# A chunk pipeline split into a front and a rear line, in the projection stage of a hybrid encoder layer

## The chip, the cores and the metric

The kernel runs on one NeuronCore of one Trainium2 chip. The metric is the device time of one execution in microseconds. Before the change three runs took 1786.5 to 1789.83 us, median 1787.34 us.

## The reference, cut to what matters

One layer of an encoder, 1024 positions of width 1024. RMSNorm, one combined projection to 26 column tiles of 128, two groups of heads that read it, an output projection, a second norm and an MLP. Tiles 0 to 11 are q, k and v of the attention heads; tiles 12 to 25 feed the recurrent heads.

```python
h = _rms_norm(x, ln1_g); proj = h @ w_in
q, k, v, u = proj[..., :512], proj[..., 512:1024], proj[..., 1024:1536], proj[..., 1536:]
attn = _dilated_window_attention(q, k, v, q_g, k_g)     # q and k are RMS-normed per head of 64
rwkv = _rwkv7_bidirectional(u, ...)                     # below
x = x + concat([attn, rwkv]) @ w_out
x = x + square(relu(_rms_norm(x, ln2_g) @ w_up)) @ w_down
...
for direction, reverse in ((0, False), (1, True)):
    decay = exp(-exp(-softplus(-(w0 + tanh(xw) @ w2)) - 0.5)); a = sigmoid(a0 + xa @ a2)
    kt = k * (1 + (a - 1) * k_a)
    # S_t = S_{t-1} (diag(w_t) - kk_t^T (a_t kk_t)) + v_t^T k_t ;  y_t = S_t r_t
    ys.append(_wkv7_scan(r, decay, kt, v, kk, a, reverse))
```

The scan is done in 16 chunks of 64 positions. What does not depend on the state (products within a chunk, the inverse of a 64x64 triangular system, values scaled by running decays) is prepared for all chunks ahead, and a short recurrence over chunks follows.

## The kernel before, in words

The kernel is one program in a framework that keeps the written order as a priority: a planner places each instruction on its engine by dependencies, buffers and that order, and each engine then runs its own queue strictly in order. DMAs are issued from the queues of SP, ScalarE (ACT) and GpSimd (POOL).

**Three stages.** `in_proj` (L164 to L635) makes the projection and the chunk preparation; `mixers` (L839 to L981) runs the recurrence over chunks with attention beside it; `tail` (L984 on) is the output projection and the MLP, 128x512 matmuls one after another.

**The dense filler.** Generator `dense` (L353) goes through the 26 column tiles in `order`. `proj` (L275) does one tile: per half of 512 positions 24 matmuls of 128x512 (three products of a high and low split, eight blocks of the contraction), with a `yield` after every six. I call six such matmuls a dense step. A half ends in `evac`: for the recurrent tiles one multiply (L308), for q and k a norm in place (L318 to L333: scale, Square on ACT, `head_inv` with eight small matmuls and a reciprocal, `head_rep` with a Sqrt on ACT and four transposes, a multiply, a split, two DMAs), for v four transposes and two DMAs (L338 to L350).

**The chunk units.** For each of four head pairs `p` and each half `hf`: `per_half` (L415) makes the normalised key `kkn`, the transposed values `VT` and the decay gate `om`; then for each direction `d` `unit_a` (L447) makes th, the exponentials EE and Ei, the scaled operands `al` and `bk` (L472 to L484), the 128x128 products `psg` (L496), masked to `G` by VectorE (L501), DMAs of G to `gd` and `rec_dr`, transposes `psb` (L508), copies `BK` (L512) and a DMA on the ACT queue (L513). `bonus` (L582) closes a half. `bk` holds three blocks per chunk; the third is a copy by ACT (L482) for the upper 64 partitions.

**The triangular systems.** When both halves of a (p, d) are done, `pair_b` (L520) goes on a list `back`: it loads the 16x16 diagonal blocks `MP` from `gd`, inverts them in 15 VectorE steps (L534, L536), stores them (`td`), and then per half loads `Ab`, `t16`, `t16t` and runs `unit_c` (L556): four rounds of 32 matmuls of 64x64 into the one bank `psd` (L564), each followed by a VectorE operation that the next round needs. The two halves run one after the other.

**The pacing.** `drive` (L386) advances a chunk generator one `yield` at a time; after each it advances `back` by 0.6 of a step and the dense filler by 0.7. `until` (L381) runs the filler until a tile is there. When all chunks are out, L630 to L633 run each remaining `back` step with four dense steps; then the stage's pools are closed and `mixers` starts, where `fill(20, 4.7)` (L965) gives each of 16 chunk steps up to 20 dense steps if any are left, else 4.7 pieces of attention.

**PSUM.** Eight banks: three `pa` for the dense accumulators, shared with the norms' and v's small products (`psq`); two `pm` (`pse`) for the chunk units' small products; two `pg` (`psg`, `psb`); one `pd` (`psd`).

Of the kernel before, what the change touches and what calls it, by code (L numbers as in the profile page):

```python
# [8 lines left out]
F32 = mybir.dt.float32  # L9
# [38 lines left out]
def tile_trunk(ctx: ExitStack, tc: tile.TileContext, xT, w_in, w_o, w_up, w_dn, vecs, w2w0, a2, g2, cst, att,  # L48
# [82 lines left out]
    def head_rep(rn, sp, pp):  # L131
        rx = sp.tile([P, 8, 64], F32, name="rx", tag="rx")
        nc.scalar.activation(rx, rn.rearrange("p (i o) -> p i o", o=1).to_broadcast([P, 8, 64]), AF.Sqrt)
        psb = pp()
        for t in range(4):
            nc.tensor.transpose(psb[:, t * P:(t + 1) * P], rx[:, 2 * t:2 * t + 2].rearrange("p h x -> p (h x)"), ident)
        return psb
# [26 lines left out]
    def in_proj():  # L164
        with ExitStack() as st:
# [24 lines left out]
            def prefetch():  # L190
                i = len(raws)
                if i < len(order):
                    r = []
                    for j in range(2):
# [5 lines left out]
                     [pa[0].tile([P, 512], F32, name="ps_u", tag="acc"), pd.tile([P, 512], F32, name="ps_u", tag="psd")],  # L200
                     [pg.tile([P, 512], F32, name="ps_u", tag="psg") for _ in range(2)]]
# [114 lines left out]
            def qk_tile(p, which):  # L316

                def evac(hf, ps):  # L318
# [9 lines left out]
                    hi = tq.tile([P, 512], F32R, name="qhi", tag="qt")  # L328
                    nc.scalar.copy(hi, qc)
                    lo = tq.tile([P, 512], F32R, name="qlo")  # L330
                    nc.vector.tensor_sub(lo, qc, r2f(hi))
                    nc.sync.dma_start((qh_dr, kh_dr)[which][p][:, sl], r2f(hi))
                    nc.sync.dma_start((ql_dr, kl_dr)[which][p][:, sl], r2f(lo))  # L333
                yield from proj(4 * which + p, evac)

            def v_tile(p):

                def evac(hf, ps):  # L338
# [4 lines left out]
                    ps = pq()  # L343
                    for t in range(4):
                        nc.tensor.transpose(ps[:, t * P:(t + 1) * P], vc[:, t * P:(t + 1) * P], ident)
                    vn = tq.tile([P, 4, 2, 65], F32, name="vn", tag="qt")
                    nc.gpsimd.memset(vn[:, :, :, 64:65], 1.0)
                    nc.scalar.copy(vn[:, :, :, 0:64], ps.rearrange("p (t h e) -> p t h e", t=4, h=2))
                    for h in range(2):
                        nc.sync.dma_start(v_dr[p][h, sl].rearrange("(t p) f -> p t f", p=P), vn[:, :, h])  # L350
                yield from proj(8 + p, evac)

            def dense():  # L353
                for c in order:
# [6 lines left out]
                    T.setdefault(c - 12, None)  # L361
# [5 lines left out]
            filler = dense()  # L367
# [18 lines left out]
            def drive(g, rate):  # L386

                while True:
                    try:
                        next(g)  # L390
                    except StopIteration as e:
                        return e.value
                    behind(0.6)
                    credit[0] += rate
                    while credit[0] >= 1.0:
                        credit[0] -= 1.0
                        next(filler, None)
# [17 lines left out]
            def per_half(w):  # L415
# [5 lines left out]
                rn = head_inv(sq, 1.0, 1e-12, up, pp)  # L421
                kkn = w["kkn"] = up.tile([P, 512], F32, name="kkn")
                nc.vector.scalar_tensor_tensor(kkn, kr[:, sl], V("kk", p), head_rep(rn, up, pp), ALU.mult, ALU.mult)
# [23 lines left out]
            def unit_a(u, w, d):  # L447
# [24 lines left out]
                al = up.tile([P, 8, 2, 64], F32, name="al")  # L472
                bk = up.tile([P, 8, 3, 64], F32, name="bk")
# [7 lines left out]
                nc.vector.scalar_tensor_tensor(bk[:, :, 0], v3(tm), 0.5, Ei, ALU.mult, ALU.mult)  # L481
                nc.scalar.copy(bk[64:128, :, 2], bk[64:128, :, 0])  # L482
                nc.vector.tensor_mul(kt, kt, kr[:, sl])
                nc.vector.tensor_mul(bk[:, :, 1], v3(kt), Ei)  # L484
                yield
                w["kt"].append(kt)
                for h in range(2):
                    nc.gpsimd.dma_start(rec_dr[d][H[h], cs, p, h * P:h * P + 64], al[H[h], :, 0])
                    nc.gpsimd.dma_start(rec_dr[d][H[h], cs, p, 448 + h * 64:512 + h * 64], al[H[h], :, 1])
                gd = dr.tile([64, 1040], F32, name=f"gd{u}")  # L490
                Gs = [up.tile([P, 8, P], F32, name="G", bufs=2) for h in range(2)]
                for g in range(2):
                    pss = [pg.tile([P, 4, P], F32, name="psg") for h in range(2)]
                    for c in range(4):
                        for h in range(2):
                            nc.tensor.matmul(pss[h][:, c], bk[H[h], 4 * g + c, h:h + 2].rearrange("p a b -> p (a b)"),  # L496
                                             al[H[h], 4 * g + c].rearrange("p a b -> p (a b)"), start=True, stop=True)
                    yield
                    for h in range(2):
                        gm = K(f"gm{'fb'[d]}{h}").rearrange("p (o x) -> p o x", o=1)  # L500
                        nc.vector.tensor_mul(Gs[h][:, 4 * g:4 * g + 4], pss[h], gm.to_broadcast([P, 4, P]))  # L501
# [698 lines left out]
```

## Time and profile before

The profiled execution took 1784.77 us, of which the span of the core's instructions is 1783.0 us and 1.77 us lie around it. Stages by the granted clock and by how much of each engine is busy (us; the windows are cut at the first products of the recurrence and at the start of the uninterrupted tail):

| stretch | length | PE | DVE | ACT | POOL | granted clock | DMA share |
|---|---|---|---|---|---|---|---|
| 0 to 60, start | 60 | 48.5 | 37.0 | 29.9 | 15.8 | 0.97 | 0.56 |
| 60 to 612, projection and chunks | 552 | 479.8 | 334.0 | 201.7 | 100.0 | 0.89 | 0.70 |
| 612 to 960, recurrence and attention | 348 | 308.1 | 191.9 | 145.1 | 64.5 | 0.93 | 0.86 |
| 960 to 1010, end of attention | 50 | 45.7 | 28.4 | 20.4 | 11.2 | 0.87 | 0.57 |
| 1010 to 1783, tail | 773 | 767.5 | 270.6 | 146.4 | 102.6 | 1.00 | 0.16 |

PE is TensorE, DVE VectorE. "Busy" is time in which an instruction of the engine was running; the clock is the mean share of full speed that TensorE was granted; the DMA share is the mean busy share of the core's 16 DMA engines.

### The profile page before, as it was taken

How to read it: one execution, taken by the hardware profiler on the slowest of the kernel's cores; microseconds unless marked ns; L12 is line 12 of the kernel's file. 1: busy time of each engine (PE TensorE's matmuls, PEld its weight loads, DVE VectorE, ACT ScalarE, POOL GpSimd, SP SyncE). 2: the span in 40 equal slices, each digit the busy share in tenths (PEclk: the TensorE clock that was granted, in tenths of full speed). 3: DMA queues.
4: the chain of work that ended last, by engine and by line, in shares of the span. 5: the costliest groups of instructions: out<-in, count | busy, mean ns of one | idle time of the engine just before them, and what ended most of it. 6: DMA issues, size and time to landing. Idle time of an engine off the chain costs nothing. (4 is left out here: it accounts for less than half of the span.)

```text
span 1783.0 us, 29922 instructions
## 1 busy us (share of the span) xinstructions
PE 1649.5 (93%) x11912; PEld 1365.7 (77%) x11912; DVE 861.9 (48%) x1754; ACT 543.5 (30%) x990; POOL 294.2 (16%) x322
## 2 busy tenths in 40 slices
PE   7999978979869997989998999999999999999999
PEld 6777767767757776877786887888888888888887
DVE  6655658757545424565775667332332233223321
ACT  5534334443412213535464234211121112112210
POOL 3022112222200000121223115200120012001200
PEclk9999989879879999988998999999999999999999
DMA  6155788878875599997973411111111111111121
GB/s 221 45 142 125 158 160 174 177 176 176 193 173 135 179 223 202 274 272 210 248 198 108 149 48 54 49 53 48 51 50 47 48 48 48 48 48 54 47 96 53
DMA packets 336923, 223.11 MB, mean 125 GB/s; under 512 B 238320, under 2 KB 289408, under 8 KB 332688
## 3 DMA queue, kind: packets, MB, share of 16 engines
q1 hardware_dynamic: 305520, 195.82, 42.7%
q10 hardware_dynamic: 27680, 15.38, 3.2%
q0 software_dynamic: 3584, 10.00, 2.5%
q8 instruction: 94, 1.54, 0.4%
q14 instruction: 45, 0.37, 0.1%
HBM read 150.22 MB, written 70.91 MB: 124 GB/s over the span
## 5 line engine op out<-in xcount | busy, mean ns | idle before, releaser
L101 ACT CAST w3h<-w3raw 128x512 fp32r<-128x512 f32 (+1 forms) x152 | 90.9, 600 | 397.0 <-PE ps L106 387.3
L106 PE MATMUL ps<-h2l,w3h 128*128 128x512 f32 x512 | 199.2, 389 | 1.1 <-DVE h2l L1045 1.1
L105 PE MATMUL ps<-h2h,w3h 128*128 128x512 f32 x512 | 199.3, 390 | 0.7 <-DVE x L1023 0.7
L107 PE MATMUL ps<-h2h,w3l 128*128 128x512 f32 x512 | 199.2, 389 | 0.0
L1089 POOL TENSOR_TENSOR relu<-relu 128x512 f32<-128x512 f32 x64 | 76.8, 1201 | 530.1 <-DVE relu L1088 530.1
L105 PE MATMUL ps_u<-hh,wh 128*128 128x512 f32 x368 | 156.1, 424 | 3.5 <-DVE ur L308 3.5
L107 PE MATMUL ps_u<-hh,wl 128*128 128x512 f32 x368 | 149.6, 407 | 0.0
L106 PE MATMUL ps_u<-hl,wh 128*128 128x512 f32 x368 | 149.3, 406 | 0.0
L102 DVE TENSOR_TENSOR w3l<-w3raw,w3h 128x512 fp32r<-128x512 f32 (+1 forms) x152 | 105.1, 693 | 79.7 <-ACT w3h L101 79.7
L1097 DVE TENSOR_TENSOR x<-x,ps 128x512 f32<-128x512 f32 x64 | 44.0, 688 | 181.7 <-PE ps L107 181.7
L105 PE MATMUL ps<-rw,w3h 128*128 128x512 f32 x320 | 124.7, 390 | 0.9 <-ACT w3h L101 0.9
L105 PE MATMUL ps<-f,w3h 128*128 128x512 f32 x320 | 124.7, 390 | 0.0
L106 PE MATMUL ps<-rw,w3h 128*128 128x512 f32 x320 | 124.5, 389 | 0.0
L107 PE MATMUL ps<-f,w3l 128*128 128x512 f32 x320 | 124.5, 389 | 0.0
L106 PE MATMUL ps<-f,w3h 128*128 128x512 f32 x320 | 124.5, 389 | 0.0
L107 PE MATMUL ps<-rw,w3l 128*128 128x512 f32 x320 | 124.1, 389 | 0.0
L106 PEld LDWEIGHTS ps<-h2l,w3h 128*128 128x128 f32 x512 | 96.1, 188 | 21.3 <-DVE h2l L1045 1.6
L105 PEld LDWEIGHTS ps<-h2h,w3h 128*128 128x128 f32 x512 | 96.1, 188 | 21.0 <-ACT w3h L101 1.1
L107 PEld LDWEIGHTS ps<-h2h,w3l 128*128 128x128 f32 x512 | 96.1, 188 | 19.9
L1088 DVE SCALAR_TENSOR_TENSOR relu<-ps,rep 128x512 f32<-128x512 f32 x64 | 44.1, 691 | 108.4 <-PE ps L107 108.2
L105 PEld LDWEIGHTS ps_u<-hh,wh 128*128 128x128 f32 x368 | 72.0, 196 | 20.2 <-DVE ur L308 4.3
L106 PEld LDWEIGHTS ps_u<-hl,wh 128*128 128x128 f32 x368 | 71.8, 195 | 16.7 <-issue 2.9
(331 smaller groups left out, 3228.7 us busy)
## 6 DMA issues: line engine op xcount, KB each, us to landing
rec<-rec_dr SPq DMA_DIRECT2D x32, 1152.0 KB, 10.0
w3raw<-in_w_up SPq DMA_DIRECT2D x64, 256.0 KB, 2.5
w3raw<-in_w_dn SPq DMA_DIRECT2D x64, 256.0 KB, 2.5
raw<-in_w_in SPq DMA_DIRECT2D x46, 256.0 KB, 2.9
rec_dr<-al POOLq DMA_DIRECT2D x64, 128.0 KB, 4.2
rec_dr<-G SPq DMA_DIRECT2D x32, 256.0 KB, 4.3
rec_dr<-G SPq DMA_DIRECT2D x64, 128.0 KB, 4.4
rec_dr<-BK ACTq DMA_DIRECT2D x16, 512.0 KB, 5.3
```

What stands on the lines that cost most here:

```text
L101: nc.scalar.copy(hi, raw)
L102: nc.vector.tensor_sub(lo, raw, r2f(hi))
L105: nc.tensor.matmul(ps, lh, rh, start=start, stop=False)
L106: nc.tensor.matmul(ps, lh, rl, start=False, stop=False)
L107: nc.tensor.matmul(ps, ll, rh, start=False, stop=stop)
L1088: nc.vector.scalar_tensor_tensor(t, pss[hf], 0.0, rep[:, HS[hf]], ALU.max, ALU.mult)
L1089: nc.gpsimd.tensor_mul(t, t, t)
L1097: nc.vector.tensor_add(x1[c][:, HS[hf]], x1[c][:, HS[hf]], ps)
```

## The change

Four things are changed, all but the pacing of `mixers` inside `in_proj`.

1. `unit_a` becomes two generators. `front` makes th, EE, al and bk and ends; `rear` takes al and bk (two buffers each now) and does the products, G, the transposes, BK and the DMAs, and at the end of the second half puts the pair on `back`. A main loop advances the line of fronts and the line of rears by one step each, then `back` by 1.0 and the filler by 1.1. A half has 14 steps instead of 22, because the rear's steps no longer stand in the fronts' line, and `per_half` has two more.
2. `bk` keeps two blocks. Each half of the partitions writes its own order: VectorE writes the first product in two operations of 64 partitions, GpSimd the second in two operations of 64 partitions. The ACT copy is gone.
3. `pair_b` loads both halves' systems, then advances two `unit_c` in turn; the second takes its bank from `pm`. `Nb` shares the buffers of `t16`, `Tp` that of `MP`.
4. The norms of q, k and the transposes of v are put on a list `late` and are advanced once after each later dense step, a norm in two parts.

PSUM becomes two `pa`, three `pm` (with `psq` in them), one `pg` of two banks, one `pd`. The end loop gives three dense steps per `back` step instead of four, and `mixers` 4.4 pieces instead of 4.7. `wb` shares the buffer of `om`, `wbh` that of `kkn`, `qlo` that of `rx`.

```diff
-            pa = [st2.enter_context(tc.tile_pool(name="pa", bufs=3, space=PSUM, reuse_waits="tile"))]
-            pq_ = [lambda: pa[0].tile([P, 512], F32, name="psq", tag="acc")]
-            pm = s1.enter_context(tc.tile_pool(name="pm", bufs=2, side="right", space=PSUM, reuse_waits="tile"))
-            pg = s1.enter_context(tc.tile_pool(name="pg", bufs=2, side="right", space=PSUM, reuse_waits="tile"))
+            pa = [st2.enter_context(tc.tile_pool(name="pa", bufs=2, space=PSUM, reuse_waits="tile"))]
+            pq_ = [lambda: pp()]
+            pm = s1.enter_context(tc.tile_pool(name="pm", bufs=3, side="right", space=PSUM, reuse_waits="tile"))
+            pg = s1.enter_context(tc.tile_pool(name="pg", bufs=1, side="right", space=PSUM, reuse_waits="tile"))
...
                     sq = tq.tile([P, 512], F32, name="qsq", tag="qt")
                     nc.scalar.activation(sq, qc, AF.Square)
-                    rn = head_inv(sq, 1.0 / HD, NORM_EPS, tq, pq)
-                    nc.vector.scalar_tensor_tensor(qc, qc, qg8 if which == 0 else V("kg"), head_rep(rn, tq, pq), ALU.mult,
-                                                   ALU.mult)
...
+                    def rest():
+                        rn = head_inv(sq, 1.0 / HD, NORM_EPS, tq, pq)
+                        rx = head_wide(rn, tq)
+                        yield
+                        nc.vector.scalar_tensor_tensor(qc, qc, qg8 if which == 0 else V("kg"), head_turn(rx, pq), ALU.mult,
+                                                       ALU.mult)
...
+                        lo = tq.tile([P, 512], F32R, name="qlo", tag="rx")
...
+                    late.append(rest())
...
+            def later():
+
+                for _ in dense():
+                    yield
+                    while late and next(late[0], 1) == 1:
+                        late.pop(0)
+                        break
...
+            filler = later()
...
+            rears, gds = [], {}
+
+            def rear_step():
+                while rears and next(rears[0], 1) == 1:
+                    rears.pop(0)
...
             def until(c):
+                n = 0
                 while c not in T:
                     next(filler)
-                    behind(0.3)
...
+                    n += 1
+                    if n % 2 == 0:
+                        rear_step()
+                        behind(0.6)
...
-            def unit_a(u, w, d):
+            def front(w, d):
...
-                bk = up.tile([P, 8, 3, 64], F32, name="bk")
+                al = up.tile([P, 8, 2, 64], F32, name="al", bufs=2)
+                bk = up.tile([P, 8, 2, 64], F32, name="bk", bufs=2)
...
-                nc.vector.scalar_tensor_tensor(bk[:, :, 0], v3(tm), 0.5, Ei, ALU.mult, ALU.mult)
-                nc.scalar.copy(bk[64:128, :, 2], bk[64:128, :, 0])
                 nc.vector.tensor_mul(kt, kt, kr[:, sl])
-                nc.vector.tensor_mul(bk[:, :, 1], v3(kt), Ei)
-                yield
+                for h in range(2):
+                    nc.vector.scalar_tensor_tensor(bk[H[h], :, h], v3(tm)[H[h]], 0.5, Ei[H[h]], ALU.mult, ALU.mult)
+                for h in range(2):
+                    nc.gpsimd.tensor_mul(bk[H[h], :, 1 - h], v3(kt)[H[h]], Ei[H[h]])
                 w["kt"].append(kt)
+                return dict(p=p, hf=hf, d=d, cs=cs, al=al, bk=bk)
+
+            def rear(v):
...
-                    pss = [pg.tile([P, 4, P], F32, name="psg") for h in range(2)]
+                    pss = pg.tile([P, 2, 4, P], F32, name="psg")
...
-                return gd
+                gds[p, d, hf] = gd
+                if hf == 1:
+                    back.append(pair_b(p * 2 + d, p, d, [gds[p, d, z] for z in range(2)]))
...
-                    yield from unit_c(dict(p=p, d=d, cs=slice(hf * 8, hf * 8 + 8), Ab=Ab, t16=t16, t16t=t16t))
+                    vs.append(unit_c(dict(p=p, d=d, hf=hf, cs=slice(hf * 8, hf * 8 + 8), Ab=Ab, t16=t16, t16t=t16t)))
+                yield
+                while vs:
+                    vs = [v for v in vs if next(v, 1) != 1]
+                    yield
...
-                    ps = v3(pd.tile([P, 512], F32, name="psd"))
+                    ps = v3(pd.tile([P, 512], F32, name="psd") if v["hf"] == 0 else pp())
...
+                        for d in range(2):
+                            rears.append(rear((yield from front(w, d))))
+                            yield
+                        yield from bonus(w)
+
+            line = fronts()
+            more = True
+            while more or rears:
+                while len(rears) > 1:
+                    rear_step()
+                if more:
+                    more = next(line, 1) != 1
+                rear_step()
+                behind(1.0)
+                credit[0] += 1.1
+                while credit[0] >= 1.0:
+                    credit[0] -= 1.0
+                    next(filler, None)
             while back:
                 behind(1.0)
-                for _ in range(4):
+                for _ in range(3):
                     next(filler, None)
...
-            fill(20, 4.7)
+            fill(20, 4.4)
```

More of the change, by code (lines that the diff above doesn't have):

```diff
@@ L199, in in_proj @@
             early = [[pa[0].tile([P, 512], F32, name="ps_u", tag="acc") for _ in range(2)],
-                     [pa[0].tile([P, 512], F32, name="ps_u", tag="acc"), pd.tile([P, 512], F32, name="ps_u", tag="psd")],
-                     [pg.tile([P, 512], F32, name="ps_u", tag="psg") for _ in range(2)]]
+                     [pm.tile([P, 512], F32, name="ps_u", tag="m"), pd.tile([P, 512], F32, name="ps_u", tag="psd")],
+                     pg.tile([P, 2, 512], F32, name="ps_u", tag="psg")]
+            early[2] = [early[2][:, hf] for hf in range(2)]
             with tc.tile_pool(name="xp", bufs=2, side="right", reuse_waits="tile") as xp:
@@ L342, in evac, with rest @@
                     nc.vector.tensor_mul(vc, ps, rep[:, sl])
[L343 to L350, printed above, removed]
+                    def rest():
+                        ps = pq()
+                        for t in range(4):
+                            nc.tensor.transpose(ps[:, t * P:(t + 1) * P], vc[:, t * P:(t + 1) * P], ident)
+                        vn = tq.tile([P, 4, 2, 65], F32, name="vn", tag="qt")
+                        nc.gpsimd.memset(vn[:, :, :, 64:65], 1.0)
+                        nc.scalar.copy(vn[:, :, :, 0:64], ps.rearrange("p (t h e) -> p t h e", t=4, h=2))
+                        for h in range(2):
+                            nc.sync.dma_start(v_dr[p][h, sl].rearrange("(t p) f -> p t f", p=P), vn[:, :, h])
+                        if hf == 1:
+                            T[8 + p - 12] = None
+                        yield
+                    late.append(rest())
                 yield from proj(8 + p, evac)
@@ L366, in in_proj @@
             T = {}
-            filler = dense()
+            late = []
+            def later():
[4 more added lines that the diff above has]
+                        break
+                while late:
+                    if next(late[0], 1) == 1:
+                        late.pop(0)
+                    yield
+            filler = later()
             credit = [0.0]
@@ L504, in unit_a @@
                     nc.sync.dma_start(mats(gd, h), Gs[h][H[h], :, 0:64])
-                pss = [pg.tile([P, 8, 64], F32, name="psb", tag="psg") for h in range(2)]
+                pss = pg.tile([P, 2, 8, 64], F32, name="psb", tag="psg")
                 for c in range(8):
                     for h in range(2):
-                        nc.tensor.transpose(pss[h][:, c], bk[H[h], c, h:h + 2].rearrange("p a b -> p (a b)"), K("id2")[H[h]])
+                        nc.tensor.transpose(pss[:, h, c], bk[H[h], c].rearrange("p a b -> p (a b)"), K("id2")[H[h]])
                 yield
@@ new lines, in fronts @@
+            def fronts():
+                for p in range(4):
+                    until(8 + p)
+                    kr, rr, vr = T[4 + p], T[p], T[8 + p]
+                    ps_ = slice(p * P, p * P + P)
+                    wr = up.tile([P, 4, P], F32, name="wr", tag="tm")
+                    for z in range(2):
+                        nc.sync.dma_start(wr[H[z], 0:2], w2w0[:, 0:64, ps_].rearrange("d k c -> k d c"))
+                        nc.sync.dma_start(wr[H[z], 2:4], a2[:, :, ps_].rearrange("d k c -> k d c"))
+                    wb = up.tile([33, 2, P], F32, name="wb", tag="om")
+                    for z in range(2):
+                        nc.sync.dma_start(wb[32 * z:32 * z + 1], w2w0[:, 64:65, ps_].rearrange("d k c -> k d c"))
+                    wh = up.tile([P, 4, P], F32R, name="wh2")
+                    nc.scalar.copy(wh, wr)
+                    nc.vector.tensor_sub(wl[0:64], wr[0:64], r2f(wh[0:64]))
+                    wbh = up.tile([33, 2, P], F32R, name="wbh", tag="kkn")
+                    nc.scalar.copy(w0s[0:1], wb[0:1])
+                    nc.scalar.copy(wbh[32:33], wb[32:33])
+                    nc.vector.tensor_sub(w0s[32:33], wb[32:33], r2f(wbh[32:33]))
+                    for hf in range(2):
+                        w = dict(p=p, hf=hf, kr=kr, rr=rr, vr=vr, wh=wh, wl=wl, kt=[])
+                        yield from per_half(w)
+                        for d in range(2):
+                            rears.append(rear((yield from front(w, d))))
+                            yield
+                        yield from bonus(w)
```

94 lines of the change are left out of this document (31 added, 63 removed).

## The prediction

> **What bounds the kernel now.** I read the page's head first, then the busy time of the stages, then TensorE's waits in the stage that the change touches, then the order of time around the longest waits.
>
> ```profile
> span 1783.0 us, 29922 instructions
> 60.00:612.00 552.00, 479.84 (x4359) 393.03 (x4359) 333.97 (x672) 201.71 (x315) 100.01 (x171) 0.89 0.70 155
> 612.00:960.00 348.00, 308.08 (x3713) 259.99 (x3709) 191.88 (x565) 145.09 (x357) 64.53 (x39) 0.93 0.86 220
> 1010.00:1783.00 773.00, 767.45 (x3402) 634.52 (x3400) 270.57 (x398) 146.41 (x240) 102.57 (x78) 1.00 0.16 53
> L106 PE MATMUL ps<-h2l,w3h 128*128 128x512 f32 x512 | 199.2, 389 | 1.1 <-DVE h2l L1045 1.1
> L106 PE MATMUL ps_u<-hl,wh 128*128 128x512 f32 x310 | 126.4, 408 | 0.0
> ```
>
> After the length, the window rows give busy PE, weight loads, DVE, ACT, POOL, then granted clock and DMA share. The tail (from 1010) is TensorE without a hole at clock 1.00; nothing there changes. The stage with the change is 60 to 612: TensorE is busy 479.84 of 552, so 72 us are holes, and the clock is 0.89. No other engine is full (DVE 334 of 552). The last two rows put a price on the slower clock: the same 128x512 matmul takes 408 ns here and 389 in the tail, 4.9% of 480, some 23 us. So 95 us are the most that a better order can win here; the matmuls themselves stay. Who makes the holes:
>
> ```profile
> PE psq L124 <- ACT qsq L324: 18.9, 10, 9.0
> PE pse L454 <- ACT om L443: 14.7, 3, 7.2
> PE psg L496 <- DVE G L501: 9.0, 7, 4.0
> PE psd L564 <- DVE Yt L576: 4.3, 4, 1.7
> PE psd L564 <- DVE bk L484: 4.2, 1, 4.2
> PE psg L496 <- DVE al L475: 3.3, 1, 3.3
> PE psg L496 <- DVE bk L484: 2.2, 3, 1.2
> PE psb L508 <- DVE G L501: 2.1, 5, 0.8
> PE psq L136 <- ACT rx L133: 1.8, 3, 1.2
> PE pse L136 <- ACT rx L133: 1.7, 1, 1.7
> ```
>
> Each row gives total, times and longest. Every one is a chain that the diff touches. But the longest have their root further back, in the order of time:
>
> ```profile
> 500.67 1.86 PE L124 MATMUL psq<-ct,qsq 128*128 128x2 f32 x8 [4.88 <-ACT qsq L324]
> 527.96 1.86 PE L124 MATMUL psq<-ct,qsq 128*128 128x2 f32 x8 [9.04 <-ACT qsq L324]
> 527.27 0.63 ACT L324 ACTIVATE qsq<-qc 128x512 f32<-128x512 f32 x1 [9.01 <-DMA kh_dr<-qhi]
> 499.01 0.16 DVE L534 TENSOR_TENSOR stmp<-Tt,MP 128x1 f32<-128x1 f32 x1 [7.39 <-DMA MP<-gd]
> 361.56 1.28 ACT L443 ACT_TABLE_LOAD   x1 [6.42 <-DMA rec_dr<-G]
> 363.50 0.79 PE L454 MATMUL pse<-xa,wh 128*128 128x512 f32 x1 [7.16 <-ACT om L443]
> DVE G L501 <- DMA rec_dr<-G: 13.4, 5, 4.1
> DVE stmp L534 <- DMA MP<-gd: 28.2, 3, 10.7
> ```
>
> The 9.04 us before L124 at 528 are ACT waiting for a DMA out of the buffer that qhi and qsq share; the 4.88 at 500 are DVE, held by the diagonal blocks; the 7.16 at 363 are ACT, held by a DMA. An order that only puts distance between written steps shortens those, but doesn't remove them.
>
> **The change part by part.** A dense step is six matmuls, of this spacing:
>
> ```profile
> 559.63 0.39 PE L106 MATMUL ps_u<-hl,wh 128*128 128x512 f32 x1
> 559.86 0.39 PE L107 MATMUL ps_u<-hh,wl 128*128 128x512 f32 x1
> ```
>
> 6 x 0.23 = 1.4 us.
>
> *Norms a step later.* Of the 18.9 us before L124 two waits make 4.88 + 9.04 = 13.9; the other eight share 5.0, 0.6 each, and vanish behind 1.4 us of dense work. The two long ones lose 1.4 each, 2.8. The waits for rx (1.8 + 1.7) get a step of their own and go. Together -11; bounds 0 and -22. Late next is ACT behind its DMA wait, as before. The two DMAs per norm move with it on SP's queue by one step, past the next weight prefetch (L196), at no cost: raw weights are asked for a tile, eight dense steps, ahead. `qlo` in rx's buffer makes the next Sqrt wait for qlo's DMA; ACT's later casts stand behind it, and a half of a tile lies between, four dense steps.
>
> *A third bank.* L454 needs only old operands, so its 14.7 us are for one of two `pm` banks that om still fills. With three it starts; but L464 behind it needs om itself, so much of the hole moves there unless dense work stands between, and the norms and second systems now use these banks too. Half: -7; bounds 0 and -14.7. The accumulators fall from three banks to two: one half (24 matmuls, 5.5 us) of cover for an evacuation that DVE delays. A hold on DVE of 10.7 us, the longest in the row above, would show, but a half of dense work is spread over more than its 5.5 us by the chunk work between. Nothing, bound +10; that holds for every loss by banks now shared (norms and second systems in `pm`).
>
> *Rear behind front.* al and bk (3.3 + 2.2), G (9.0 + 2.1) are 16.6 us. The 4.0 us wait is G's own buffers waiting for their DMA; these stay two. Counting steps, the rear line is empty when a d=0 unit ends, so that unit's products follow in the same pass; only d=1 units, half of 16, get distance. Half of 12.6: -6; bounds 0 and -16.6.
>
> *Two systems in turn.* The Yt waits, 4.3, go: the other half's 32 matmuls stand between. The 4.2 us (DVE behind a memset) stay. `Ab` keeps one buffer, so its second load still stands on SP behind the first half's product, with t16 loads queued behind it, as now. -4; bounds 0 and -8.5.
>
> Sum of holes: -28 of 72. *Clock:* in proportion to the holes, 28/72 of 23, -9; bounds 0 and -23. The stretch without a long wait is why I take the proportion:
>
> ```profile
> 320.00:340.00 20.00, 17.66 (x134) 14.46 (x135) 14.40 (x33) 6.93 (x12) 10.70 (x17) 0.66 0.81 171
> 323.50 0.33 PE L564 MATMUL psd<-t,Ab 64*64 64x64 f32 x2 [2.19 <-DMA t<-td]
> ```
>
> Here the clock is 0.66 though the longest wait is 2.19 us. The Trainium skill (TensorE: Matmul & The Clock Gate, "Why this matters for your kernels") says that only idle gaps of over some 3 us take the clock back to half. By it the clock term would be near 0, as the long waits mostly stay, and the sum 9 us higher; this slice speaks against it.
>
> *bk on POOL and DVE.*
>
> ```profile
> L474 POOL TENSOR_TENSOR al<-us,EE x16: 1170/1383/2238, 98.4 to 484.6; 128x512 f32<-128x512 f32 x16
> L481 DVE SCALAR_TENSOR_TENSOR bk<-tm,Ei x16: 675/688/1686, 98.9 to 489.0; 128x512 f32<-128x512 f32 x16
> L484 DVE TENSOR_TENSOR bk<-kt,Ei x16: 676/682/1671, 100.5 to 489.6; 128x512 f32<-128x512 f32 x16
> L481 DVE SCALAR_TENSOR_TENSOR bk<-tm,Ei 128x512 f32<-128x512 f32 x16 | 15.9, 994 | 1.8 <-PE psb L508 1.8
> L482 ACT COPY bk<-bk 64x512 f32<-64x512 f32 x16 | 9.9, 616 | 11.5 <-DVE bk L481 11.4
> L615 DVE TENSOR_TENSOR wl<-wr,wh 64x512 fp32r<-64x512 f32 x3 | 2.1, 684 | 2.2 <-ACT wh L614 2.2
> ```
>
> Half the partitions cost the whole time (684 ns for 64x512). DVE: 0.69 + 0.68 out at the medians, 2 x 0.68 in, nothing. ACT loses 16 x 0.62, off the path. POOL gets 32 x 1.38 = 44 us (1.17 to 2.24 each). The path to a product was 0.68 + 0.62 and becomes 2 x 1.38, +1.5: hidden in the d=1 units, in eight d=0 units partly covered by dense work, +6; bounds 0 and 16 x 1.5 = +24. L481 lies at 688 median and 994 mean, up to 1686 where L474 runs at the same time: each POOL operation now costs DVE 0.3 us on average and 1.0 at worst. 32 x 0.3 = 10 us on DVE, of which, DVE being 60% busy, I put a third on the path: +3; bounds 0 and +32.
>
> *Shared buffers at the head of each p* (wb behind om, wbh behind kkn): three starts, a load each; the readers are done steps earlier. +2; bounds 0 and +7.
>
> *Dense work moved.* I counted steps in the code. Before: a half has 3 + 2 x 9 + 1 = 22 chunk steps, eight halves 176, x 0.7 = 123, and 22 come from `until`: 145 of 214; the end loop's 21 x 4 take the rest. After: 8 x 14 and four for the last rear are 116, x 1.1 = 127, and 22: 149; 16 x 3 in the end loop make 197 of 215. So 18 go to `mixers`, which gets 18 x 1.4 = 25 us of TensorE work more and the stage so much less. `mixers` has 40 us of holes (348 - 308) under a 0.86 DMA share; I let it absorb a fifth, -5; bounds 0 and -25.
>
> Sum: -28 - 9 + 6 + 3 + 2 - 5 = -31. Against the profiled execution (1783.0 span and 1.77 around it, 1784.8) 1753.8; the median of the runs, 1787.3, is 2.5 higher, so **1756**. All gains at their bounds: -62 (holes) - 23 - 25 = -110, 1677; nobody gets all.
>
> **Rivals.**
>
> *The stall only moves to the DMAs.* For: 28.2 and 13.4 us of DVE and 9.0 and 6.4 of ACT wait for DMAs, their number and queues stay, and a shorter stage asks them for more per us. Against: the stage's share is 0.70, that of the next 0.86. Then only the short waits go (5 + 3.5 + 4): 1787 - 12, with the clock as it is and POOL's +6 to +9 against it: 1775 to 1784, say 1780.
>
> *Slower: POOL holds DVE and bk.* At full price the two POOL terms are 24 + 32 = 56 instead of 9: -31 + 47 = +16, 1803. It turns at two thirds of that price (31 of 47). For: the 1686 and 1671 above, and POOL's queue also holds the al DMAs. The Trainium skill (SBUF — State Buffer, "Who interferes with whom") says that a DVE operation with two SBUF inputs and a GpSimd one that reads SBUF exclude each other for the whole of one; the maxima agree. Against: means lie near the median in L484, and POOL is busy 100 of 552.
>
> *Much more:* if the DMA waits are covered too, half of what is left of the 95 comes as well: 1715.
>
> *The change does nothing,* since a planner orders the queues:
>
> ```profile
> L106 PE MATMUL ps_u<-hl,wh x368: 387/389/799, 53.1 to 667.7; 128*128 128x512 f32 x184
> L886 PE MATMUL psY<-rec,pv x512: 221/222/369, 612.2 to 951.8; 128*64 128x64 f32 x171
> ```
>
> By the written order all dense work precedes the recurrence, yet it ends at 667.7, after the latter's start. Against: buffers, banks and operations change as well. 1787.
>
> **How the numbers follow.** Forecast 0.50 (1738 to 1774), DMA 0.17, slower 0.20, much more 0.08, nothing 0.05. The range leaves out most of "much more" and the upper half of "slower": 1722 to 1800. About 0.2%, 3.6 us, is what a measurement can tell: faster is forecast, much more and most of DMA (0.50 + 0.08 + 0.12 = 0.70); same the rest of DMA and nothing (0.10); slower 0.20.
>
> **What would show it.** Right: the stage up to the recurrence ends near 560, 50 us earlier (25 moved, 26 won); L124's waits under 10 us, Yt's gone, clock above 0.90; the waits for DMAs still there. Wrong: waits of L496 for a POOL bk over 20 us, or L481's mean over 1.2 us (slower); waits with a DMA at their root as long in sum as before (DMA); a recurrence over 400 us long, which would give the moved work back.

## The result, and the profile after

The changed kernel takes 1900.9 us (median of four runs, 1888.7 to 1905.0), the kernel before 1788.6 beside it: ratio 1.062, 95% interval 1.059 to 1.065. The forecast was 1756, the range 1722 to 1800. The profiled execution took 1901.22 us.

The page of the changed kernel begins so (length; then busy us, share and instructions of each engine):

```profile
span 1899.4 us, 29998 instructions
PE 1680.4 (88%) x11912; PEld 1392.0 (73%) x11912; DVE 888.4 (47%) x1754; ACT 542.3 (29%) x980; POOL 349.9 (18%) x354
```

The windows, cut at nearly the same places of the work as before (start of the chunks, first product of the recurrence, last one, start of the tail; the tail's window holds 46 matmuls, some 10 us, more than before):

```profile
60.00:736.00 676.00, 528.61 (x4477) 430.70 (x4476) 376.70 (x682) 202.06 (x312) 154.55 (x206) 0.85 0.58 130
736.00:1054.00 318.00, 274.89 (x3479) 234.11 (x3479) 162.21 (x510) 129.21 (x323) 54.76 (x31) 0.87 0.92 232
1116.00:1899.00 783.00, 777.99 (x3448) 643.17 (x3446) 276.92 (x413) 149.72 (x246) 110.72 (x85) 1.00 0.17 54
346.00:437.50 91.50, 54.52 (x721) 46.70 (x721) 51.69 (x86) 21.93 (x34) 34.33 (x41) 0.73 0.65 130
```

The recurrence begins at 736 where it began at 612. The stage of the change has become 124 us longer: 75 us of that are holes (147 where 72 were), 49 are TensorE busier (528.6 against 479.8), by a lower clock (0.85 against 0.89) and by 92 dense matmuls, 21 us at 0.23, that ran beside the recurrence before (144 there, now 52). The last row is one stretch in it, of which more below. TensorE's waits from 60 to 736 (total, times, longest):

```profile
PE psd L604 <- DMA t<-td: 25.9, 9, 10.1
PE ps_u L105 <- DVE qc L326: 21.2, 13, 3.4
PE psg L529 <- DVE G L534: 20.4, 7, 6.0
PE psg L529 <- POOL bk L513: 9.6, 7, 2.3
PE pse L604 <- DMA Ab<-gd: 8.2, 2, 7.9
```

The waits for qsq and om that led the list before are gone from its top, as meant. Those for Yt are smaller, not gone (3.3 us where 4.3 were), and waits for Nb in the same systems, 0.3 before, come to 8.6. In their place stand loads of the triangular systems, and a wait that did not exist: dense matmuls (L105) that wait for VectorE to evacuate an accumulator (`qc`).

**Two places show where the time went.** The first is the norm of the first q half. In the order of time (start, duration, engine, line, operation, and in brackets the idle time before it and its releaser):

```profile
338.45 0.70 DVE L326 TENSOR_TENSOR qc<-ps_u,acc 128x512 f32<-128x512 f32 x1
339.19 0.63 ACT L328 ACTIVATE qsq<-qc 128x512 f32<-128x512 f32 x1 [6.02 <-DVE qc L326]
...
345.42 0.39 PE L107 MATMUL ps_u<-hh,wl 128*128 128x512 f32 x1
...
421.51 1.04 PE L124 MATMUL pse<-ct,qsq 128*128 128x2 f32 x8
...
435.57 0.68 DVE L339 TENSOR_TENSOR qlo<-qc,qhi 128x512 fp32r<-128x512 f32 x1
436.73 0.69 DVE L326 TENSOR_TENSOR qc<-ps_u,acc 128x512 f32<-128x512 f32 x1
437.48 0.80 PE L105 MATMUL ps_u<-hh,wh 128*128 128x512 f32 x1 [1.31 <-DVE qc L326]
```

The half's square is ready at 339.8, but its eight small products (L124) run at 421.5, 82 us later. Until `qlo` has read `qc`, at 436.3, the next half can't be evacuated, since `tq` holds one `qc`; the next two halves fill both accumulators by 345.8 (31 halves are multiplied by then, and only the 29th is evacuated); and so TensorE has no dense matmul for 92 us. In that stretch only chunk work runs, with nothing between its links: 54.5 us busy of 91.5, at clock 0.73 (the window above). What stands ahead of L124 in TensorE's queue there are the products of two pairs, fronts and rears. Waits for the loads `t` and `Ab` make 13.5 of the 37 us of holes.

The second place is the end, where few chunk steps are left. Evacuations, the norm and the dense work between them:

```profile
657.48 0.69 DVE L326 TENSOR_TENSOR qc<-ps_u,acc 128x512 f32<-128x512 f32 x1
658.22 0.79 PE L105 MATMUL ps_u<-hh,wh 128*128 128x512 f32 x1 [3.02 <-DVE qc L326]
658.82 0.63 PE L106 MATMUL ps_u<-hl,wh 128*128 128x512 f32 x1
659.24 0.63 PE L107 MATMUL ps_u<-hh,wl 128*128 128x512 f32 x1
...
665.00 0.40 PE L107 MATMUL ps_u<-hh,wl 128*128 128x512 f32 x1
665.69 0.95 PE L124 MATMUL pse<-ct,qsq 128*128 128x2 f32 x8
...
670.37 0.69 DVE L339 TENSOR_TENSOR qlo<-qc,qhi 128x512 fp32r<-128x512 f32 x1 [0.74 <-ACT qhi L337]
671.10 0.69 DVE L326 TENSOR_TENSOR qc<-ps_u,acc 128x512 f32<-128x512 f32 x1
671.84 0.79 PE L105 MATMUL ps_u<-hh,wh 128*128 128x512 f32 x1 [3.40 <-DVE qc L326]
```

From evacuation to evacuation 13.6 us pass, and the chain fills them: L124 starts 8.2 us after the evacuation, `qlo` ends 5.4 later, and the next evacuation follows at once. The kernel before, same kind of half:

```profile
582.14 0.69 DVE L322 TENSOR_TENSOR qc<-ps_u,acc 128x512 f32<-128x512 f32 x1 [3.29 <-PE ps_u L107]
583.60 1.05 PE L124 MATMUL psq<-ct,qsq 128*128 128x2 f32 x8 [0.42 <-ACT qsq L324]
588.42 0.69 DVE L331 TENSOR_TENSOR qlo<-qc,qhi 128x512 fp32r<-128x512 f32 x1 [0.69 <-ACT qhi L329]
592.05 0.69 DVE L322 TENSOR_TENSOR qc<-ps_u,acc 128x512 f32<-128x512 f32 x1 [1.60 <-PE ps_u L107]
```

There the chain ends after 7.0 us, and VectorE waits for the last matmul of the next half, not TensorE for VectorE: a half takes 9.9 us. The stretch from the last psg product to the recurrence has grown from 106 to 150 us. It holds 10.8 halves of dense work where 9.0 were: by this count nine of them 3 us slower are about 28 of the 44 us, and the 1.8 halves more are left to make the rest.

### The profile page after: what moved, and what is told of

Read it like the earlier page. It is cut to its first block, busy times and chain, and to the rows that moved or that the text cites. A ratio compares the mean times of both kernels' runs of the same rounds, so it can differ in the third digit from the quotient of the medians.

```text
span 1899.4 us, 29998 instructions
## 1 busy us (share of the span) xinstructions
PE 1680.4 (88%) x11912; PEld 1392.0 (73%) x11912; DVE 888.4 (47%) x1754; ACT 542.3 (29%) x980; POOL 349.9 (18%) x354
## 5 line engine op out<-in xcount | busy, mean ns | idle before, releaser
L105 PE MATMUL ps<-h2h,w3h 128*128 128x512 f32 x512 | 199.3, 390 | 0.6 <-DVE x L1075 0.6
L105 PE MATMUL ps_u<-hh,wh 128*128 128x512 f32 x368 | 156.5, 425 | 26.2 <-DVE qc L326 21.2
L106 PE MATMUL ps_u<-hl,wh 128*128 128x512 f32 x368 | 155.2, 422 | 0.0
L107 PE MATMUL ps_u<-hh,wl 128*128 128x512 f32 x368 | 153.5, 417 | 0.0
L105 PE MATMUL ps<-rw,w3h 128*128 128x512 f32 x320 | 124.7, 390 | 0.9 <-ACT w3h L101 0.9
L105 PE MATMUL ps<-f,w3h 128*128 128x512 f32 x320 | 124.7, 390 | 0.0
L105 PEld LDWEIGHTS ps<-h2h,w3h 128*128 128x128 f32 x512 | 96.1, 188 | 21.0 <-ACT w3h L101 1.0
L105 PEld LDWEIGHTS ps_u<-hh,wh 128*128 128x128 f32 x368 | 74.9, 203 | 45.5 <-DVE qc L326 23.6
L107 PEld LDWEIGHTS ps_u<-hh,wl 128*128 128x128 f32 x368 | 74.8, 203 | 17.2 <-issue 1.0
```

Source lines behind the costliest of these rows:

```text
L105: nc.tensor.matmul(ps, lh, rh, start=start, stop=False)
L106: nc.tensor.matmul(ps, lh, rl, start=False, stop=False)
L107: nc.tensor.matmul(ps, ll, rh, start=False, stop=stop)
```

## The experiments

Each was timed beside the kernel before on its chip. Differences between two edits below are of their medians; by their ratios to the kernel before they come out up to 6 us otherwise. First the four parts, each taken back alone.

**Norms at once** (`for _ in rest(): pass` in place of `late.append(rest())`, in both places).

> The changed kernel with the norms of q and k and the transposes of v done at once in the evacuation again; banks, lines and systems stay as changed. Theory A (the later norms together with two accumulators lock the dense line to the norm chain: a half is evacuated, a half of dense work runs, and only then come the norm's eight small matmuls, so that the next evacuation waits for the whole chain): the pitch of a half in the end loop falls from 13.4 us to about 10, waits of the first dense matmul for DVE's qc from 21 us to under 8, the kernel to about 1860. Rival B (two accumulators alone are too few): pitch stays over 12, kernel within 10 us of 1901.

1897.9 us, ratio 1.059 (1.054 to 1.064). That the norms are written a step later is not what cost the 112 us: the square of the first q half still waits 81 us for its L124. At the end, too, L124 still starts 7.5 us after an evacuation (663.19 to 670.66), and the halves follow each other every 12.5 us, where I had expected 10.

**Three accumulators, two banks in the pool.**

```diff
-pa bufs=2 ... pm bufs=3
+pa bufs=3 ... pm bufs=2
```

> The changed kernel with three accumulator banks and two for the small products, which norms, second systems and chunk units share. Theory A: dense work can go on during a norm, so the end loop's pitch falls to about 10 us and the kernel to 1850 to 1870; the chunk phase (first to last product of a unit, 98 to 586 us) stays as long or gets longer by waits for the two shared banks. Rival B predicts the same end loop; this run tells A and B apart only together with the one before.

1928.5 us, ratio 1.077 (1.074 to 1.080), the slowest of all, where I had expected 1850 to 1870. The scarce banks here are those of the pool `pm`, not the accumulators.

**One system after the other**, both in `psd`, each half's loads written with its first product.

```diff
-                    vs.append(unit_c(...))
-                yield
-                while vs:
-                    vs = [v for v in vs if next(v, 1) != 1]
-                    yield
+                    yield from unit_c(...)
...
-ps = v3(pd.tile(..., name="psd") if v["hf"] == 0 else pp())
+ps = v3(pd.tile(..., name="psd"))
```

> The changed kernel with the two halves' triangular systems one after the other in the one bank psd again, their loads in the same step as the first product as before. Theory C (12 loads at once and the earlier place of the first products make TensorE wait for t and Ab, 34 us, and stretch the chunk phase): waits of psd for t and Ab fall under 8 us, the chunk phase from 488 us to about 455, the kernel to about 1865. Rival D (the chunk phase is stretched by the rear line itself, G written again right after its DMAs were issued): chunk phase stays over 475, kernel 1885 to 1910.

1813.1 us, ratio 1.013 (1.010 to 1.016): 88 of the 112 us are in this part.

**All of bk on VectorE** (`nc.vector.tensor_mul` in place of `nc.gpsimd.tensor_mul`).

> The changed kernel with the second product of bk on VectorE instead of GpSimd (two operations of 64 partitions). Theory E (GpSimd's products hold VectorE and come late to the products): waits of psg for bk fall from 9.6 us to under 3, the kernel by 15 to 30 us to 1870 to 1885. Rival D: within 8 us of 1901, since 22 us more of work on VectorE cancel it.

1896.4 us, ratio 1.060 (1.057 to 1.063): nothing. The price of the shared engines was real, though. The groups of the changed kernel, and then those of this run (busy us, mean ns):

```profile
L513 POOL TENSOR_TENSOR bk<-kt,Ei 64x512 f32<-64x512 f32 x32 | 51.9, 1623 | 1.2
L511 DVE SCALAR_TENSOR_TENSOR bk<-tm,Ei 64x512 f32<-64x512 f32 x32 | 39.9, 1246 | 4.2 <-ACT Ei L494 3.8
```

```profile
L511 DVE SCALAR_TENSOR_TENSOR bk<-tm,Ei 64x512 f32<-64x512 f32 x32 | 30.6, 956 | 0.3
```

VectorE's product took 1246 ns with GpSimd's beside it and 956 without, 9 us in all. But VectorE also got the other 32 products, 27 us of work. So the run shows that the exchange is worth nothing, not what the 9 us alone are worth.

Then the 88 us were taken apart. Theory F: the second system takes its bank from the pool, and fronts and norms stand behind it. Theory G: the single `Ab` puts a load in the middle of the pair. Theory H: the pair's products come too close together.

**A bank of its own** for the second system, `pm` with two banks.

```diff
-pm bufs=3
+pm bufs=2
-ps = v3(pd.tile(..., name="psd") if v["hf"] == 0 else pp())
+ps = v3(pd.tile(..., name="psd", tag="psd" if v["hf"] == 0 else "psd1"))
```

> The changed kernel, but the second half's system multiplies in a bank of its own; the pool that fronts, norms and second systems shared keeps two of its three banks, for fronts and norms alone. The systems still advance in turn. Theory F (the second system, while it stands behind its loads, holds a bank that the fronts and the norms take in order, so that the fronts and the dense line behind them stop): 1810 to 1835, as with one system after the other (1813). Theory G (the single Ab buffer puts the second half's load in the middle of the pair): no change, 1885 to 1905. Theory H (only the packing of the pair's eight products back to back counts): no change, 1885 to 1905. Fewer banks for the norms alone, as where the pool had two of the three: 1915 to 1930.

1864.7 us, ratio 1.043 (1.036 to 1.049): between the theories. The square of the first q half waits 78 us for its L124 here too, with no system in the pool.

**One Ab.** The second load of `Ab` is left out, and the second half multiplies with the first half's.

> The changed kernel, but the second half's systems multiply with the first half's Ab; the second load of Ab is left out, so the second half's systems are computed from other data. No product of the pair waits for an Ab load that is issued in its middle. Theory G: 1815 to 1845. Theory F: 1880 to 1900, the bank is held as long. Theory H: 1885 to 1905.

1897.4 us, ratio 1.060 (1.057 to 1.063). Theory G falls. **Both edits:**

> Both edits: second system in a bank of its own and no second Ab load (the second half's systems are computed from the first half's Ab). Theories F or G: as the better of the two alone, 1805 to 1840. If each alone moves nothing and both together do, the stall has two holds in parallel: 1805 to 1840 here only. Theory H (the packing of the pair's products, not what they wait for): 1880 to 1905.

1867.3 us, ratio 1.043 (1.039 to 1.046), as with the bank alone, although that wait is 47 us here in place of 78.

**One after the other, and norms at once.**

> One system after the other (as in the run that gave 1813) and also the norms written at once in place of a dense step later. If the rest of the loss against the kernel before (some 23 us) is the pitch of the dense line at its end, where each half waits for the chain of norms: 1790 to 1800. If the norms are not its cause: 1808 to 1818.

1834.3 us, ratio 1.025 (1.022 to 1.029): a miss. Here norms a step later are 21 us better than norms in place.

**Loads first, then one after the other**, one `Ab` (second load left out).

```diff
-                while vs:
-                    vs = [v for v in vs if next(v, 1) != 1]
-                    yield
+                for v in vs:
+                    yield from v
```

> The changed kernel with the loads of both halves' systems written first, as the change has them, and a step between loads and products, but the systems one after the other in the one bank. The second load of Ab is left out (both halves multiply with the first half's Ab), since one buffer holds it. With one system after the other and the loads split the time was 1813; with both in turn, the second in a bank of its own, 1865, with or without the second Ab load. If the loads written together (up to twelve in one step) are what the remaining 50 us come from: 1850 to 1870. If it is the products in turn: 1805 to 1825.

1832.4 us, ratio 1.024 (1.021 to 1.026): between the two, 19 us over the run without.

**The pace of the pairs:** 0.75 in place of 1.0 with systems in turn and a bank of their own; 1.3 with one after the other.

> The second system in a bank of its own, in turn, and the pairs advanced by 0.75 of a step in each pass of the main loop in place of 1.0, so that the ten steps of a pair take 13 passes, about as many as a pair has where the systems follow one another. Theory H as pace (the products of a pair come too close together because a pair has fewer steps): 1815 to 1840. Theory H as turns (two products with nothing between them in each step, however far the steps lie apart): 1855 to 1875.

> One system after the other, and the pairs advanced by 1.3 of a step per pass in place of 1.0, so that the twelve steps of a pair take some nine passes. Theory H as pace: 1840 to 1870. Theory H as turns: 1800 to 1820, below 1813 if the longer end loop (164 us, where 106 stood before) is a backlog of pairs that this shortens.

1873.3 us, ratio 1.046 (1.044 to 1.049), and 1851.5 us, ratio 1.035 (1.029 to 1.040). Slower pairs don't mend the turns, faster pairs spoil the sequence by 38 us; neither form of theory H expected both.

**One after the other, banks as before** (three `pa`, which the norms share, two `pm`).

> One system after the other, and the banks dealt as before: three accumulators, which the norms share, and two banks for the fronts' small products. Front and rear lines, bk without the third block and norms a step later stay. If the banks that norms and fronts now share cost the rest (1813 against 1789): 1780 to 1798. If they do not, the fronts lose the third bank and the time is 1815 to 1835.

1841.8 us, ratio 1.029 (1.027 to 1.032), above both ranges.

**One after the other, one pool bank idle** (`pm` 2, nothing else), and **in turn in one bank** (both systems in `psd`, `pm` 3).

> One system after the other (1813), with one of the three banks of the fronts and norms taken away and left idle. If the third bank is worth much also where no second system uses it: 1835 to 1860; then the loss that stayed where the second system had its own bank (1865) is mostly that bank. If two banks do: 1808 to 1820, and the loss that stayed there is the turns.

> The changed kernel, two systems in turn, but both in the one bank of the first system; the fronts and norms keep three banks for themselves. If the turns cost only by the shared pool and the loads written first: 1825 to 1840, as one after the other with the loads first (1832). If the turns themselves cost: 1850 to 1875.

1839.9 us, ratio 1.031 (1.028 to 1.035), and 1838.1 us, ratio 1.029 (1.026 to 1.033). The second is the run that gives theory F its price: the changed kernel with one line edited, so that the second system's bank no longer comes from the pool, is some 60 us faster (63 by the medians, 58 by the ratios), and in turn or one after the other (with the loads first) differ by 6. The own bank had cost one of the pool's three, which alone is worth 27. The first q half of this run, in the order of time:

```profile
327.77 0.63 ACT L328 ACTIVATE qsq<-qc 128x512 f32<-128x512 f32 x1 [7.40 <-DVE qc L326]
...
354.02 1.03 PE L124 MATMUL pse<-ct,qsq 128*128 128x2 f32 x8
```

26 us from the square to its products, not 82. Its stage up to the first product of the recurrence:

```profile
60.00:693.80 633.80, 515.65 (x4471) 417.90 (x4471) 374.60 (x682) 202.31 (x314) 153.01 (x207) 0.88 0.66 148
```

The recurrence begins at 694, 42 us before the changed kernel's, with holes of 118 us in place of 147. The other 20 us of the 60 come behind that point, where the edited line no longer runs; no run here tells why.

**Norms and banks alone on the kernel before.**

> The kernel before with two things of the change alone: norms a step later, and two accumulators with a pool of three banks for fronts and norms. Chunk units in one line, bk with three blocks and the systems one after the other stay as before. If these two help as they did in the changed kernel with one system after the other (21 and 28 us): 1740 to 1765. By the prediction's terms (-11 and -7): 1768 to 1780. If their gain there only mended what the lines broke: 1785 to 1800.

1823.6 us, ratio 1.022 (1.018 to 1.025), above all three ranges. **The two lines alone** (norms at once, banks as before, one system after the other; bk and the pace of the change).

> The front and the rear line with their pace and with bk of two blocks, but one system after the other, norms in place, banks as before (the norms in the accumulators' three). If the lines themselves cost: 1835 to 1870, as the runs that took one of the other parts back gave 1834 and 1842. If they are neutral and each other part costs: 1785 to 1800.

1793.1 us, ratio 1.0045 (1.0024 to 1.0066). Its end, evacuation by evacuation:

```profile
592.00 0.69 DVE L326 TENSOR_TENSOR qc<-ps_u,acc 128x512 f32<-128x512 f32 x1 [3.30 <-PE ps_u L107]
601.90 0.69 DVE L326 TENSOR_TENSOR qc<-ps_u,acc 128x512 f32<-128x512 f32 x1 [1.60 <-PE ps_u L107]
611.75 0.69 DVE L326 TENSOR_TENSOR qc<-ps_u,acc 128x512 f32<-128x512 f32 x1 [3.29 <-PE ps_u L107]
621.65 0.69 DVE L326 TENSOR_TENSOR qc<-ps_u,acc 128x512 f32<-128x512 f32 x1 [1.60 <-PE ps_u L107]
```

The pitch is 9.9 again and VectorE waits for TensorE.

**A measure for small terms:** the kernel before with its dense filler at 0.8 in place of 0.7, and the lines alone at 1.3 in place of 1.1.

> The kernel before with its dense filler at 0.8 of a step per chunk step in place of 0.7, nothing else. If the stage is insensitive to the mere place of its dense work: 1782 to 1792. If any other order costs as much as the small terms found: outside that, by 6 us or more; then the 6 and 7 us found for the turns and the lines say nothing of these parts.

> The lines alone (1793: norms in place, banks as before, one system after the other), with 1.3 dense steps per pass in place of 1.1. If the holes of the main loop are short of dense work: 1772 to 1788, below the kernel before. If they are waits that dense work does not cover: 1788 to 1800, and less dense work is left to the recurrence.

1808.4 us, ratio 1.011 (1.008 to 1.013), and 1833.6 us, ratio 1.025 (1.023 to 1.027). Both slower, by 19 and 40 us, with no operation added or removed; the second lies above both ranges. So a step of 20 us between two of these kernels, or of 40, may be only another place of the same work. Where the 40 us went the windows tell, up to the first product of the recurrence and from there on (each time the lines alone, then with more dense work):

```profile
60.00:631.40 571.40, 479.76 (x4384) 392.58 (x4384) 373.69 (x681) 195.95 (x303) 150.68 (x206) 0.89 0.68 153
60.00:672.60 612.60, 522.62 (x4536) 424.74 (x4536) 379.67 (x689) 199.95 (x311) 155.58 (x211) 0.88 0.64 145
631.40:1791.90 1160.50, 1112.66 (x7321) 928.74 (x7316) 482.43 (x1028) 310.45 (x637) 178.68 (x125) 0.97 0.38 108
672.60:1830.70 1158.10, 1095.15 (x7167) 918.66 (x7163) 478.41 (x1020) 311.57 (x633) 178.37 (x120) 0.95 0.38 107
```

The holes of the stage are the same (92 and 90 us). TensorE is 43 us busier in it, 30 of them by 129 dense matmuls that stood beside the recurrence before; and from the recurrence on only 2 us come back for them. The kernel before at its other pace shows the same on a smaller scale: 72 matmuls, 17 us, are moved, the recurrence begins 25 us later, and 1 us comes back. It is no rule for all these kernels: norms and banks alone leave the recurrence no dense work either, and there 40 us come back (1131 us from its first product to the end, 1171 before).

The runs side by side. "No dense" is the longest stretch from 300 us on without a dense matmul; "lag" the time from the end of the first q half's square to its L124; "pitch" the mean of the last four spacings of the q and k evacuations; "start" the first product of the recurrence, all from the order of time.

| kernel | us | no dense | lag | pitch | start |
|---|---|---|---|---|---|
| before | 1789 | 24.8 | 0.3 | 9.9 | 612 |
| lines alone | 1793 | 48.5 | 2.5 | 9.9 | 631 |
| before, other pace | 1808 | 21.9 | 0.0 | 10.1 | 637 |
| one after the other | 1813 | 12.2 | 14.2 | 12.9 | 667 |
| before + norms and banks | 1824 | 40.1 | 48.2 | 14.3 | 697 |
| one after the other, loads first | 1832 | 38.6 | 51.7 | 12.6 | 695 |
| lines, more dense | 1834 | 20.8 | 0.1 | 10.4 | 673 |
| one after the other, norms at once | 1834 | 22.4 | 14.2 | 12.5 | 687 |
| in turn, one bank | 1838 | 29.4 | 25.6 | 13.2 | 694 |
| one after the other, a bank idle | 1840 | 48.8 | 39.4 | 12.5 | 696 |
| one after the other, banks as before | 1842 | 50.3 | 5.3 | 11.2 | 682 |
| one after the other, faster pairs | 1852 | 32.3 | 7.8 | 14.0 | 686 |
| in turn, own bank | 1865 | 79.5 | 78.0 | 14.5 | 722 |
| in turn, own bank, one Ab | 1867 | 49.1 | 46.9 | 15.1 | 713 |
| in turn, own bank, slower pairs | 1873 | 59.7 | 63.6 | 14.3 | 714 |
| bk on VectorE, else changed | 1896 | 83.6 | 72.4 | 13.1 | 730 |
| one Ab, else changed | 1897 | 81.5 | 70.6 | 12.7 | 723 |
| norms at once, else changed | 1898 | 91.6 | 81.3 | 12.5 | 728 |
| changed | 1901 | 92.1 | 81.7 | 13.0 | 736 |
| two pool banks, else changed | 1928 | 89.4 | 89.6 | 12.3 | 749 |

The pitch parts the kernels cleanly: 9.9 to 10.4 where the norms stand at once and take their banks from the accumulators, 11.2 and more in all others. The lag and the stretch without dense work are long in all the slowest, but they are no price: own bank and own bank with one Ab take the same time with a lag of 78 and of 47 us. The lines with more dense work are at 1834 with neither fault.

## Why the prediction was wrong

**The step that failed** is a sentence under "A third bank": "Nothing, bound +10; that holds for every loss by banks now shared (norms and second systems in `pm`)." Second systems in `pm` measured some 60 us (1901 against 1838), 42 of them before the recurrence begins (736 against 694). I priced a shared bank as a late evacuation, one half of cover. What the changed kernel's trace shows is a chain: the norm's first product comes behind products of which some wait for DMAs, and a norm that can't end holds the only `qc`, then both accumulators, then the dense line, which was the cover of every other wait. The price is shown; that the shared bank acts by this chain alone is not. With a bank of its own, but only two pool banks, the lag is still 78 us, at 1865: a pool short of banks for fronts and norms makes the chain too.

**Norms a step later, -11.** The waits for ACT fell further than forecast (L124 waits 1.3 us in all for qsq, where 11 of the 18.9 were to stay), but "Late next is ACT behind its DMA wait" was wrong: next is the evacuation, because of the one `qc`, which I did not look up. The delay is not all of it: with the norms at once and the banks dealt as changed the pitch is 12.5, with the norms late and the banks as before 11.2, with neither 9.9. I also wrote that the two DMAs move at no cost, without pricing the chain from evacuation to `qlo`. It went from 7.0 to 13.6 us at the end and became the bound; the new L105 waits are 21.2 us. On SP's queue, too, the norms' DMAs now stand longer for qhi (52.7 us in all, 28.9 before). Norms and banks alone cost the kernel before 38 us, and 20 where the lines are there as well (1813 against 1793); neither is more than the 19 and 40 us that another pace costs.

**Third bank, -7.** The wait for om that it was meant for fell from 14.7 to some 4 us. A bank of the pool is worth 27 us where all three are for fronts and norms (1840 against 1813). But the whole new deal of banks gained 29 us with the norms late (1842 to 1813) and cost 41 with the norms at once (1793 to 1834), so the term's sign is not shown.

**Rear behind front, -6.** Not seen: the lines alone are 7 us slower, a size that another pace exceeds. In the changed kernel G's waits (9.0 before) stood at 20.4.

**Two systems in turn, -4.** Yt's waits shrank by 1 us instead of going, those for Nb grew by 8, and loads came on top: 25.9 us for `t`, 8.2 for `Ab`, where I had "as now". The turns themselves are worth 6 us, the loads written first 19; both lie within what another pace does. The second `Ab` load, which I named, cost nothing.

**Clock, -9.** It went the other way, with the holes: 0.85 against 0.89.

**bk, +9.** The sign that I had named for it came (mean over 1.2 us: 1246 ns), and yet the runs with and without GpSimd's share agree within 5 us. So the slower rival had the right side and, as far as this exchange shows, the wrong cause; at 9.6 us its other sign (over 20) did not come. The Trainium skill (SBUF — State Buffer, "Who interferes with whom") agrees with these times (1246 ns beside GpSimd's products, 956 without); that it sets the end is not shown, as VectorE was busy 47% of the span.

**Dense moved, 18 steps or 25 us to `mixers`.** It went the other way: 92 matmuls, 15 steps, came from the recurrence into the stage. The dense line stood still for 92 us and was made up in the end loop, and the recurrence began after it. The recurrence is 22 us shorter for it (318 against 340), but from its first product to the end of the kernel only 7 us come back (1164 against 1171). I had let `mixers` absorb a fifth of what moves in; the two runs at another pace took 17 and 30 us of dense work out of it and got 1 and 2 back, so there it had absorbed nearly all.

**The DMA rival** (1780) had a point: `t` and G waits have DMAs at their root and grew. It took them as constant; without dense work between, they are exposed.

What stays open: why norms late and the bank deal cost 41 and 49 us when only one of them is on the lines (1834 and 1842 against 1793) and 20 together; by which way the shared bank costs its 60 us where the lag doesn't price it; and why the recurrence gives the time of dense work back in some of these kernels (40 us with norms and banks alone) and not in others. No run takes the shared buffers (+2) apart. No version beat the kernel before.

## What to carry to other kernels

Before two kinds of work share a pool of banks, write down what the holder of a bank waits for: if it is a DMA, the other kind may now stand behind that DMA too. Before a step is delayed, or its banks are dealt anew, count the buffers between it and its producer: with a single one, the delay becomes the producer's pitch. And before a small term is believed, time a run that changes nothing but the pace, and look from which stage it takes its work: here that alone was worth 1 to 2%.

## What the runs showed of the hardware

Slow matmuls followed idle times of 2 to 3 us. In the changed kernel, in the order of time:

```profile
718.44 1.15 PE L604 MATMUL pse<-Yt,Nb 64*64 64x64 f32 x32
721.97 0.83 PE L358 MATMUL pse<-ct,vc 128*128 128x128 f32 x4 [2.38 <-DVE vc L353]
...
723.02 0.63 PE L106 MATMUL ps_u<-hl,wh 128*128 128x512 f32 x1
723.45 0.63 PE L107 MATMUL ps_u<-hh,wl 128*128 128x512 f32 x1
...
725.86 0.39 PE L107 MATMUL ps_u<-hh,wl 128*128 128x512 f32 x1
726.08 0.39 PE L105 MATMUL ps_u<-hh,wh 128*128 128x512 f32 x1
```

After 2.38 us of idle time the matmuls stand 0.43 us apart in place of 0.23, for some 3 us; after the 3.02 us at 658 they do so for over 5 us. After 1.39 us, at 709, none is slow, and after idle times under 1 us none of the dense rows that followed within 4 us lasted over 0.5 us. The rule that I weighed (the Trainium skill, TensorE: Matmul & The Clock Gate, "Why this matters for your kernels": pauses of over about 3 us take the clock back to half) holds in kind, with a shorter pause here. After the waits of 1.9 to 3.4 us at the halves' starts from 592 on, the slow matmuls thus cost another 1.5 to 2.9 us each time.
